# Two transformer blocks on one core: the value slab with the gates in one bank of each pool, its pieces cut 2, 3 and 3

## The chip, the cores and the metric

The kernel runs on one core of one Trainium2 chip, as one program in one launch. The metric is device time in microseconds (us), the median of several executions. Before the change three executions gave 802.09, 802.58 and 803.4 us, so the median is 802.58 us. Engines are named as the profile names them: PE is TensorE (PEld its weight loads), DVE is VectorE, ACT is ScalarE, POOL is GpSimd, and SP is the queue that issues nearly all DMAs.

## The reference

Two blocks run one after the other on 256 tokens of width 1024, all in float32. The first block has differential attention, retention, a squared-ReLU MLP and a gated embedding. The second block has an mLSTM mixer and a gated MLP with a causal convolution of width 3. A last RMS norm closes it. The change touches the entry of the mLSTM mixer only:

```python
def rmsnorm(x, g):
    xf = x.astype(jnp.float32)
    y = xf * lax.rsqrt(jnp.mean(xf * xf, axis=-1, keepdims=True) + EPS) * g.astype(jnp.float32)
    return y.astype(x.dtype)

def mlstm_mixer(x, w_in, b_gates, head_norm, w_out):
    ...
    proj = x @ w_in                      # 1024 -> 512 q, 512 k, 1024 v, 1024 o, 4 + 4 gates
    q = proj[..., :i0].astype(jnp.float32) * (dqk ** -0.5)
    k = proj[..., i0:i1].astype(jnp.float32)
    v = proj[..., i1:i2].astype(jnp.float32)
    o_gate = jax.nn.sigmoid(proj[..., i2:i3].astype(jnp.float32))
    log_i = proj[..., i3:i4].astype(jnp.float32) + bg[:MLSTM_HEADS]
    log_f = jax.nn.log_sigmoid(proj[..., i4:].astype(jnp.float32) + bg[MLSTM_HEADS:])
    ...
```

The eight gate columns give, by running sums and running maxima over the tokens, the decay matrix that weighs q·k before it meets v.

## The kernel before

**Slabs and pieces.** `_plan` cuts every weight matrix into slabs, mostly 8 blocks of 128 rows by 256 columns. A slab comes in pieces: `_rows` says which blocks of rows belong to each. Nearly all slabs have two pieces of four blocks, 128x1024 elements and 512 KB each. The slab `mv0` is wider: 256 columns of v and the 8 gate columns, 264 in all, which is why it has three pieces. The list `order` is the sequence of all pieces; a few pairs of slabs (`JOINT`) have their pieces interleaved. `_packed` lays the weights out in DRAM piece by piece by the same `_rows`.

**A piece's way.** SP loads the piece into one of 5 `raw` buffers (`dma_to`, L155). ACT copies it rounded into one of 6 `hi` buffers (`high_to`, L167). DVE subtracts to get the rest into one of 6 `lo` buffers (`split_to`, L179) and so frees the `raw` buffer, which lets SP load the piece five places on. PE then makes three products per block: weights hi by activations hi, hi by the activations' low part, lo by hi. All engines take their instructions in program order, so an instruction that waits holds back what stands behind it on its engine.

**Order of issue.** `halves` issues the products of a slab piece by piece. After the first piece it runs what is due in the middle (`tails` and the `mid` hooks) and then `slot`, which issues the splits of the pieces ahead and one step of every pending epilogue. `after` does the same at the slab's end.

**PSUM.** The pool `psum` has two rings of 4 banks: `mmbank` ("big products", one bank per slab) and `aux` (everything small: sums, transposes, decay, scores). A new tile takes the bank that was handed out four tiles earlier in its ring, and PE has to wait until that one has been read out.

**The place of the change.** `joint(["mq0", "mk0"], ...)` multiplies the new activations h4 into `ps_mq0` and `ps_mk0`. `step_wide("mv0")` follows, with one bank for each half of the tokens, `ps_mv0_0` and `ps_mv0_1`. After the first piece of `mv0` the tail of the joint step runs: two matmuls with `ones` (`r4_pe`, L1004 and L1005, tile `pv_n4`) sum the squares `sqs_n4` and `sqs_n5`. From them DVE and ACT make the two norms' common factor `rr` (`r4_post`, L1012 to L1020). Only then can DVE read out `ps_mq0` and `ps_mk0`, which need `rr` (`post_scaled`, L561, into `mqk`). Then come `mq1`, `mk1`, `mv1`, `mv2`, `mv3`, `mo0` and so on.

**The gates.** In the middle of `mq1`, `mv0_tail` transposes `rr` to a column on PE (`pc_c5`, L500), DVE copies it (`rrc`, L507), and ACT scales the gate columns of `ps_mv0_0` and `ps_mv0_1` into `gtok` (L1039). In the middle of `mk1` PE transposes them (`pg_t`, L1044). DVE adds the biases (`gi`, `gf`, L1051 and L1052). After `mk1`, `gates2` runs the scans on DVE (L1062 to L1071) and an exponential on ACT (`me`, L1072). After `mv1`, PE transposes `gi` and `me` to columns (`pa_g`, L1082). After `mv2` PE spreads the decay over the tokens (`mm0`, `mm1`, L1100) and makes the first scores (`ms`); DVE builds `dm` from them (L1109).

Of the kernel before, what the change touches and what calls it, by code (L numbers as in the profile page):

```python
# [37 lines left out]
def _plan():  # L38
# [47 lines left out]
    for i in range(len(slabs)):  # L86
        n = slabs[i][0]
        if n not in paired:
            order += [(i, s) for s in range(len(_rows(slabs[i])))]
        elif any(n == g[0] for g in JOINT):  # L90
            order += [(i, 0), (i + 1, 0), (i, 1), (i + 1, 1)]
# [3 lines left out]
def _rows(slab):  # L95

    name, w, k0, nk, cl = slab
    return ((0, 1, 2), (3, 4, 5), (6, 7)) if name == "mv0" else (tuple(range(nk // 2)), tuple(range(nk // 2, nk)))


def _width(slab):
    return 264 if slab[0] == "mv0" else 2048 // slab[3]
# [3 lines left out]
def block_kernel(ctx: ExitStack, tc: tile.TileContext, I, out):  # L106
# [15 lines left out]
    def mmbank(name):  # L122
        return psum.tile([P, 512], F32, tag="mm", name=name)

    def aux(name):
        return psum.tile([P, 512], F32, tag="aux", name=name)
# [10 lines left out]
    slabs, index, order = _plan()  # L137
# [7 lines left out]
    def geometry(i):  # L145
        return len(_rows(slabs[i])[0]), _width(slabs[i])

    def dma_to(n):
        while state["dma"] < min(n, len(order)):
            i, s = order[state["dma"]]  # L150
            name = slabs[i][0]
            kk, cw = len(_rows(slabs[i])[s]), _width(slabs[i])
            raw = wpool.tile([P, 1024], F32, tag="raw", name=f"raw_{name}_{s}", bufs=NRAW)
            v = raw[:, 0:kk * cw].rearrange("p (k n) -> p k n", k=kk)
            nc.sync.dma_start(out=raw[:, 0:kk * cw], in_=I["w"][state["dma"], :, 0:kk * cw])  # L155
            raw_t[i, s] = v
            state["dma"] += 1
# [100 lines left out]
    def after(i, *posts):  # L258

        if i in hooks_pe:  # L260
            drain(i - 1)
            for f in hooks_pe.pop(i):
                f()
        slot()
        for f in list(posts) + hooks_post.pop(i, []):
            later(i, f)

    def halves(i, piece):
        for s in range(len(_rows(slabs[i]))):
            need(i, s)  # L270
            piece(s)
            used.add((i, s))
            if s == 0:
                while tails and i >= tails[0][0]:
                    tails.pop(0)[1]()
                if i in hooks_mid:
                    drain(i - 1)
                    for f, g in hooks_mid.pop(i):
                        f()
                        later(i, g)  # L280
                slot()
# [23 lines left out]
    def step_wide(name, xh, xl):  # L305

        i = index[name]
        kk, cw = geometry(i)
        pss = [mmbank(f"ps_{name}_{t}") for t in range(2)]

        def piece(s):
            for t in range(2):
                ts = slice(t * P, (t + 1) * P)
                for a, k in enumerate(_rows(slabs[i])[s]):
                    hv, lv = hi_t[i, s], lo_t[i, s]
                    o = pss[t][:, 0:cw]
                    TE.matmul(o, lhsT=xh[:, k, ts], rhs=hv[:, a, :], start=k == 0, stop=False, skip_group_check=True)
                    TE.matmul(o, lhsT=xl[:, k, ts], rhs=hv[:, a, :], start=False, stop=False, skip_group_check=True)
                    TE.matmul(o, lhsT=xh[:, k, ts], rhs=lv[:, a, :], start=False, stop=k == 7, skip_group_check=True)

        halves(i, piece)
        after(i)
        return pss
# [42 lines left out]
    with tc.manual_schedule():  # L366
# [93 lines left out]
        for n in range(4):  # L460
            for tag, dt, d in (("hi", F32R, hi_t), ("lo", F32R, lo_t)):
                t = wpool.tile([P, 1024], dt, tag=tag, name=f"{tag}_{n}", bufs=NBUF)
# [262 lines left out]
        i, ps0 = index["q0"], [mmbank(f"ps_{n}") for n in ("q0", "k0")]  # L725
# [192 lines left out]
        for j in range(4):  # L918
            ps = mmbank(f"ps_f2_{j}")
            for kg in range(4):  # L920
                i = index[f"f2_{j}_{kg}"]
# [13 lines left out]
        i = index["wp"]  # L935
# [271 lines left out]
        drain(STAT - 1)  # L1207
        joint(["mq0", "mk0"], h4h, h4l, r4_pe, r4_post, [post_scaled(mqt, 0, rrq), post_scaled(mkt, 0, rr)])
        pss0 = step_wide("mv0", h4h, h4l)
        tails.append((index["mq1"], lambda: mv0_tail(pss0)))  # L1210
        step_b("mq1", h4h, h4l, post_scaled(mqt, 1, rrq))
# [316 lines left out]
```

## Time and profile before

| what | value |
|---|---|
| median of 3 executions | 802.58 us |
| the profiled execution | 802.1 us |
| its span in the profile | 800.3 us |
| PE busy | 786.9 us, 98% of the span |
| DVE busy | 569.9 us, 71% |
| ACT busy | 464.7 us, 58% |
| HBM traffic | 139.68 MB read, 1.05 MB written |
| mean granted PE clock | 0.997 of full speed |

A PE matmul of the usual form is shown with about 281 ns, but matmuls are pipelined: from one start to the next pass about 0.118 us. So stretches of PE are measured from start to start. The span lies 1.8 us below the execution's own time; that rest is outside the program's instructions.

### The profile page before, as it was taken

The numbers are of one execution on the slowest core, as the hardware profiler recorded it, in microseconds if no ns is written. First come the engines' busy times: TensorE is split into PE (matmuls) and PEld (weight loads), VectorE is DVE, ScalarE is ACT, GpSimd is POOL, SyncE is SP. The second block draws the span as 40 slices with busy tenths as digits, with TensorE's granted clock in tenths as the row PEclk, the third lists the DMA queues.
The fourth block names the chain that finished last, engine by engine and source line by source line (L and its number), as shares of the span: only waits on it lengthen the run. The fifth ranks groups of instructions, "written<-read, shape, count | busy, mean of one in ns | idle before, by whom it ended". The sixth has DMA issues, their size and how long they took to land.

```text
span 800.3 us, 15703 instructions
## 1 busy us (share of the span) xinstructions
PE 786.9 (98%) x6394; PEld 772.5 (97%) x6394; DVE 569.9 (71%) x895; ACT 464.7 (58%) x788; POOL 2.2 (0%) x8
## 2 busy tenths in 40 slices
PE   8999999999999999999999999799999999999996
PEld 8999999999999999999999999799999999999885
DVE  6877888556666667666545557887978988987443
ACT  7655657765744446556344456755865766766332
POOL 0000000000000000000000000000000000000000
PEclk9999999999999999999999999999999999999999
DMA  8775544455656556665656544354365456765621
GB/s 302 270 240 158 158 159 130 134 169 169 191 184 187 182 184 188 187 185 194 192 184 186 188 160 149 132 186 156 107 220 175 134 183 219 232 207 162 209 79 53
DMA packets 40472, 141.75 MB, mean 177 GB/s; under 512 B 4640, under 2 KB 5024, under 8 KB 40400
## 3 DMA queue, kind: packets, MB, share of 16 engines
q1 hardware_dynamic: 40032, 140.02, 55.3%
q8 instruction: 50, 0.82, 0.4%
q0 software_dynamic: 224, 0.72, 0.2%
q14 instruction: 22, 0.18, 0.1%
q10 hardware_dynamic: 144, 0.00, 0.0%
HBM read 139.68 MB, written 1.05 MB: 176 GB/s over the span
## 4 chain that ended last, share of the span: by engine, by line
PE 95%; ACT 2%; DMA 1%; DVE 1%; issue 0%; SPq 0%; DVEq 0%; ACTq 0%
PE ps_f L231 8%; PE ps_f L230 8%; PE ps_f L232 8%; PE ps_uv L230 3%; PE ps_ug L230 3%; PE ps_ug L231 3%; PE ps_uv L231 3%; PE acc L1368 3%; PE acc L1366 3%; PE acc L1367 3%; PE ps_ug L232 3%; PE ps_uv L232 3%; PE ps_vr L242 1%; PE ps_va L242 1%; PE ps_mo L242 1%; PE ps_wo L231 1%
## 5 line engine op out<-in xcount | busy, mean ns | idle before, releaser
L179 DVE TENSOR_TENSOR lo_f<-raw_f,hi_f 128x1024 fp32r<-128x1024 f32 x64 | 77.7, 1223 | 52.8 <-ACT hi_f L167 52.8
L167 ACT ACTIVATE hi_f<-raw_f 128x1024 fp32r<-128x1024 f32 x64 | 67.6, 1060 | 79.6 <-PE ps_f L231 70.3
L231 PE MATMUL ps_f<-al,hi_f 128*128 128x256 f32 x256 | 72.1, 282 | 0.0
L230 PE MATMUL ps_f<-ah,hi_f 128*128 128x256 f32 x256 | 72.0, 281 | 0.0
L232 PE MATMUL ps_f<-ah,lo_f 128*128 128x256 f32 x256 | 72.0, 281 | 0.0
L230 PE MATMUL ps_f<-h2h,hi_f 128*128 128x256 f32 x256 | 71.9, 281 | 0.0
L231 PE MATMUL ps_f<-h2l,hi_f 128*128 128x256 f32 x256 | 71.9, 281 | 0.0
L232 PE MATMUL ps_f<-h2h,lo_f 128*128 128x256 f32 x256 | 71.8, 281 | 0.0
L230 PEld LDWEIGHTS ps_f<-ah,hi_f 128*128 128x128 f32 x256 | 48.3, 189 | 0.0
L232 PEld LDWEIGHTS ps_f<-ah,lo_f 128*128 128x128 f32 x256 | 48.3, 189 | 0.0
L230 PEld LDWEIGHTS ps_f<-h2h,hi_f 128*128 128x128 f32 x256 | 48.3, 189 | 0.0
L231 PEld LDWEIGHTS ps_f<-al,hi_f 128*128 128x128 f32 x256 | 48.2, 188 | 0.0
L231 PEld LDWEIGHTS ps_f<-h2l,hi_f 128*128 128x128 f32 x256 | 48.1, 188 | 0.0
L232 PEld LDWEIGHTS ps_f<-h2h,lo_f 128*128 128x128 f32 x256 | 48.1, 188 | 0.0
L179 DVE TENSOR_TENSOR lo_dn<-raw_dn,hi_dn 128x1024 fp32r<-128x1024 f32 x22 | 26.9, 1223 | 22.8 <-ACT hi_dn L167 22.8
L167 ACT ACTIVATE hi_dn<-raw_dn 128x1024 fp32r<-128x1024 f32 x22 | 23.3, 1061 | 30.7 <-PE acc L1367 24.5
L230 PE MATMUL ps_ug<-h7h,hi_ug 128*128 128x256 f32 x144 | 40.8, 283 | 0.0
L230 PE MATMUL ps_uv<-h7h,hi_uv 128*128 128x256 f32 x144 | 40.5, 282 | 0.0
L231 PE MATMUL ps_uv<-h7l,hi_uv 128*128 128x256 f32 x144 | 40.3, 280 | 0.0
L231 PE MATMUL ps_ug<-h7l,hi_ug 128*128 128x256 f32 x144 | 40.3, 280 | 0.0
L232 PE MATMUL ps_ug<-h7h,lo_ug 128*128 128x256 f32 x144 | 40.0, 278 | 0.0
L232 PE MATMUL ps_uv<-h7h,lo_uv 128*128 128x256 f32 x144 | 40.0, 278 | 0.0
(492 smaller groups left out, 2936.6 us busy)
## 6 DMA issues: line engine op xcount, KB each, us to landing
raw_f<-in_w_dram SPq DMA_DIRECT2D x64, 512.0 KB, 4.2
raw_ug<-in_w_dram SPq DMA_DIRECT2D x22, 512.0 KB, 4.4
raw_uv<-in_w_dram SPq DMA_DIRECT2D x22, 512.0 KB, 4.3
raw_dn<-in_w_dram SPq DMA_DIRECT2D x22, 512.0 KB, 3.6
raw_va<-in_w_dram SPq DMA_DIRECT2D x8, 512.0 KB, 4.8
raw_vr<-in_w_dram SPq DMA_DIRECT2D x8, 512.0 KB, 3.5
raw_gr<-in_w_dram SPq DMA_DIRECT2D x8, 512.0 KB, 3.5
raw_ga<-in_w_dram SPq DMA_DIRECT2D x8, 512.0 KB, 3.6
```

The costliest lines, as they stand in the source:

```text
L167: S.activation(hi_t[i, s], raw_t[i, s], ACTF.Copy)
L179: V.tensor_tensor(out=lo_t[i, s], in0=raw, in1=hi_t[i, s].bitcast(F32), op=ALU.subtract)
L230: TE.matmul(o, lhsT=hv[:, a, sl], rhs=xh[:, x, :], start=st, stop=False, skip_group_check=True)
L231: TE.matmul(o, lhsT=hv[:, a, sl], rhs=xl[:, x, :], start=False, stop=False, skip_group_check=True)
L232: TE.matmul(o, lhsT=lv[:, a, sl], rhs=xh[:, x, :], start=False, stop=sp, skip_group_check=True)
L242: TE.matmul(o, lhsT=xh[:, k, ts], rhs=hv[:, a, :], start=st, stop=False, skip_group_check=True)
L1366: TE.matmul(o, lhsT=gh[b][:, r, ts], rhs=hv[:, 0, ns], start=k == 0, stop=False)
L1367: TE.matmul(o, lhsT=gl[b][:, r, ts], rhs=hv[:, 0, ns], start=False, stop=False)
L1368: TE.matmul(o, lhsT=gh[b][:, r, ts], rhs=lv[:, 0, ns], start=False, stop=k == NK - 1)
```

## The change

`ps_mv0_1` is taken from the ring `aux` in place of `mmbank`; `ps_mv0_0` stays in `mmbank`. The pieces of `mv0` hold blocks (0, 1), (2, 3, 4), (5, 6, 7) in place of (0, 1, 2), (3, 4, 5), (6, 7). The width now comes from `_width`, which gives the same 264. No instruction is added or removed on any engine.

```diff
 def _rows(slab):
 
     name, w, k0, nk, cl = slab
-    return ((0, 1, 2), (3, 4, 5), (6, 7)) if name == "mv0" else (tuple(range(nk // 2)), tuple(range(nk // 2, nk)))
+    return ((0, 1), (2, 3, 4), (5, 6, 7)) if name == "mv0" else (tuple(range(nk // 2)), tuple(range(nk // 2, nk)))
...
     def step_wide(name, xh, xl):
 
         i = index[name]
-        kk, cw = geometry(i)
-        pss = [mmbank(f"ps_{name}_{t}") for t in range(2)]
+        cw = _width(slabs[i])
+        pss = [mmbank(f"ps_{name}_0"), aux(f"ps_{name}_1")]
```

In the rows of the program's order below, a name ends in the number of its buffer, and what an instruction waits for stands in brackets.

On PE, after the first piece of `mv0` (its last products are those of `hi_mv0_0` and `lo_mv0_0`), the two sums `pv_n4` follow; this is the difference there:

```order
 L318 MATMUL ps_mv0_1_6302<-hi_mv0_0_6102,h4l_5833 128x264
 L319 MATMUL ps_mv0_1_6302<-lo_mv0_0_6123,h4h_5832 128x264
-L317 MATMUL ps_mv0_1_6302<-hi_mv0_0_6102,h4h_5832 128x264
-L318 MATMUL ps_mv0_1_6302<-hi_mv0_0_6102,h4l_5833 128x264
-L319 MATMUL ps_mv0_1_6302<-lo_mv0_0_6123,h4h_5832 128x264
-L1004 MATMUL pv_n4_6321<-sqs_n4_6199,ones_95 128x256
-L1005 MATMUL pv_n4_6321<-sqs_n5_6205,ones_95 128x256
+L1004 MATMUL pv_n4_6315<-sqs_n4_6199,ones_95 128x256
+L1005 MATMUL pv_n4_6315<-sqs_n5_6205,ones_95 128x256
 L317 MATMUL ps_mv0_0_6301<-hi_mv0_1_6187,h4h_5832 128x264
```

Three products for each half of the tokens, six in all, have gone from ahead of the two sums to the end of `mv0`.

On PE, from the last product of `mv0` to the first ones of `mq1`, and on to the transposes and the first products of `mk1`, before:

```order
L319 MATMUL ps_mv0_1_6302<-lo_mv0_2_6237,h4h_5832 128x264
L230 MATMUL ps_mq1_6382<-h4h_5832,hi_mq1_0_6253 128x256 [waits DVE_49,PE_49,Activation_49]
L231 MATMUL ps_mq1_6382<-h4l_5833,hi_mq1_0_6253 128x256
L232 MATMUL ps_mq1_6382<-h4h_5832,lo_mq1_0_6255 128x256
...
L500 MATMUL pc_c5_6407<-ident_109,rr_6128 128x128 x2
...
L230 MATMUL ps_mk1_6461<-h4h_5832,hi_mk1_0_6338 128x256 [waits DVE_49,PE_49,Activation_49]
```

and on PE at the same place of the changed kernel:

```order
L319 MATMUL ps_mv0_1_6302<-lo_mv0_2_6237,h4h_5832 128x264
L230 MATMUL ps_mq1_6382<-h4h_5832,hi_mq1_0_6253 128x256 [waits Activation_49]
L231 MATMUL ps_mq1_6382<-h4l_5833,hi_mq1_0_6253 128x256
L232 MATMUL ps_mq1_6382<-h4h_5832,lo_mq1_0_6255 128x256 [waits DVE_49]
...
L500 MATMUL pc_c5_6407<-ident_109,rr_6128 128x128 [waits DVE_49]
...
L230 MATMUL ps_mk1_6461<-h4h_5832,hi_mk1_0_6332 128x256 [waits DVE_49,Activation_49]
```

The first product of `mq1` no longer waits for DVE to read a bank out; the third now waits for its `lo` piece, the transposes wait for `rr`, and `mk1` waits for the read-out of `ps_mq0`.

On DVE, behind the two sums of squares `sqs_n4` and `sqs_n5`, this is the difference:

```order
 L435 TENSOR_TENSOR sqs_n5_6205<-sqa_n5_5835 128x256
 L179 TENSOR_TENSOR lo_mv0_1_6207<-raw_mv0_1_5972,hi_mv0_1_6187 128x792
-L179 TENSOR_TENSOR lo_mv0_2_6237<-raw_mv0_2_6007,hi_mv0_2_6235 128x528
+L179 TENSOR_TENSOR lo_mv0_2_6237<-raw_mv0_2_6007,hi_mv0_2_6235 128x792
 L179 TENSOR_TENSOR lo_mq1_0_6255<-raw_mq1_0_6039,hi_mq1_0_6253 128x1024
 L179 TENSOR_TENSOR lo_mq1_1_6297<-raw_mq1_1_6076,hi_mq1_1_6295 128x1024
```

The third piece is larger here by one block of 264 columns, and `lo_mv0_0`, ahead of these rows, is smaller by one. No instruction changes its place on DVE, ACT or SP.

## Rows read from the trace of the kernel before

**Rows 1.** The page: first its line of engines (busy us, share of the span, instructions), then the chain of work that ended last, by engine.

```profile
PE 786.9 (98%) x6394; PEld 772.5 (97%) x6394; DVE 569.9 (71%) x895; ACT 464.7 (58%) x788; POOL 2.2 (0%) x8
...
PE 95%; ACT 2%; DMA 1%; DVE 1%; issue 0%; SPq 0%; DVEq 0%; ACTq 0%
```

**Rows 2.** The waits of PE over the whole span: who waited for whom, us in total, times, longest us.

```profile
PE ps_mq L230 <- ACT hi_mv L167: 3.8, 1, 3.8
...
PE ps_q L230 <- ACT hi L466: 0.9, 2, 0.6
PE ps_mq L230 <- ACT h4h L441: 0.6, 1, 0.6
```

**Rows 3.** The timeline of PE from `mv0` to `mv2`: start us, duration us, engine, line, tiles, shape, and in brackets the idle time before and what ended it. The buffers' numbers are left out, so `mq0` and `mq1` are both `mq`; here it is `mq1`, `mk1`, `mv1` and `mv2`.

```profile
515.02 0.28 PE L319 MATMUL ps_mv<-lo_mv,h4h 128*128 128x264 f32 x1
519.06 0.55 PE L230 MATMUL ps_mq<-h4h,hi_mq 128*128 128x256 f32 x1 [3.76 <-ACT hi_mv L167]
...
522.17 0.28 PE L232 MATMUL ps_mq<-h4h,lo_mq 128*128 128x256 f32 x1
...
523.24 0.28 PE L232 MATMUL ps_mq<-h4h,lo_mq 128*128 128x256 f32 x1
523.36 0.38 PE L500 MATMUL pc_c<-ident,rr 128*128 128x128 f32 x2
...
526.41 0.28 PE L230 MATMUL ps_mk<-h4h,hi_mk 128*128 128x256 f32 x1
...
529.25 0.38 PE L1044 MATMUL pg_t<-ident,gtok 128*64 128x128 f32 x2
...
538.11 0.22 PE L1082 MATMUL pa_g<-ident,gi 4*128 4x4 f32 x1
538.19 0.20 PE L1082 MATMUL pa_g<-ident,me 4*128 4x4 f32 x1
```

**Rows 4.** Stretches of the span: length us, then busy us and instructions of PE, PEld, DVE, ACT and POOL, then the granted clock of PE as a share of 2.4 GHz, the DMA share and GB/s.

```profile
515.20:519.10 3.90, 0.14 (x2) 0.07 (x1) 2.80 (x8) 3.78 (x6) 0.00 (x0) 0.95 0.81 295
519.10:522.20 3.10, 3.10 (x15) 3.10 (x16) 2.68 (x3) 0.84 (x1) 0.00 (x0) 0.51 0.22 26
522.20:538.00 15.80, 15.80 (x135) 15.77 (x134) 12.29 (x20) 8.04 (x16) 0.00 (x0) 1.00 0.67 230
```

**Rows 5.** The timeline of DVE in the same stretch, columns as in rows 3.

```profile
499.26 0.98 DVE L179 TENSOR_TENSOR lo_mv<-raw_mv,hi_mv 128x792 fp32r<-128x792 f32 x1
500.15 0.69 DVE L982 TENSOR_TENSOR pgs<-pgs,pw 128x512 f32<-128x512 f32 x1
...
509.92 0.43 DVE L435 TENSOR_TENSOR sqs_n<-sqa_n 128x256 f32<-128x256 f32 x1
510.27 1.59 DVE L179 TENSOR_TENSOR lo_mv<-raw_mv,hi_mv 128x792 fp32r<-128x792 f32 x2
511.78 2.35 DVE L179 TENSOR_TENSOR lo_mq<-raw_mq,hi_mq 128x1024 fp32r<-128x1024 f32 x2
...
517.43 0.42 DVE L402 TENSOR_TENSOR rr<-nt_n,y_n 128x256 f32<-128x256 f32 x1
...
518.22 0.69 DVE L561 TENSOR_TENSOR mqk<-ps_mq,rrq 128x512 f32<-128x512 f32 x1
...
519.42 2.35 DVE L179 TENSOR_TENSOR lo_mk<-raw_mk,hi_mk 128x1024 fp32r<-128x1024 f32 x2
523.77 0.16 DVE L507 COPY rrc<-pc_c 128x2 f32<-128x2 f32 x1 [2.00 <-PE pc_c L500]
...
529.67 0.47 DVE L1051 TENSOR_SCALAR gi<-pg_t,par 4x256 f32<-4x256 f32 x1 [0.93 <-PE pg_t L1044]
...
530.66 2.36 DVE L179 TENSOR_TENSOR lo_mv<-raw_mv,hi_mv 128x1024 fp32r<-128x1024 f32 x2
```

**Rows 6.** The timeline of ACT: the first and the third piece of `mv0` with what follows each, and the exponential of the gates.

```profile
492.99 0.87 ACT L167 ACTIVATE hi_mv<-raw_mv 128x792 fp32r<-128x792 f32 x1 [1.18 <-PE ps_pg L231]
493.77 1.69 ACT L441 ACTIVATE h4h<-x,gfg 128x256 fp32r<-128x256 f32 x4
...
509.07 0.63 ACT L167 ACTIVATE hi_mv<-raw_mv 128x528 fp32r<-128x528 f32 x1
509.60 1.99 ACT L167 ACTIVATE hi_mq<-raw_mq 128x1024 fp32r<-128x1024 f32 x2
...
536.69 0.42 ACT L1072 ACTIVATE me<-gl 4x256 f32<-4x256 f32 x1 [3.25 <-DVE gl L1071]
```

**Rows 7.** The timeline of PE in the joint step and in `mv0`, columns as in rows 3.

```profile
501.30 0.28 PE L232 MATMUL ps_mk<-h4h,lo_mk 128*128 128x256 f32 x1
502.16 0.38 PE L230 MATMUL ps_mq<-h4h,hi_mq 128*128 128x256 f32 x1 [0.58 <-ACT h4h L441]
...
508.46 0.29 PE L317 MATMUL ps_mv<-hi_mv,h4h 128*128 128x264 f32 x1
...
510.64 0.59 PE L1004 MATMUL pv_n<-sqs_n,ones 128*128 128x256 f32 x2
...
511.31 0.47 PE L317 MATMUL ps_mv<-hi_mv,h4h 128*128 128x264 f32 x1
```

**Rows 8.** From issue to landing of the five loads of `raw_mv` (512 KB each) that are issued between 511 and 525 us.

```profile
DMA to landing us min/median/max: 3.6/4.8/5.1
```

**Rows 9.** The timeline of DVE after the decay products of PE, columns as in rows 3.

```profile
545.14 2.69 DVE L1109 SCALAR_TENSOR_TENSOR dm<-mm,acol,maskT 128x256 f32<-128x256 f32 x8 [1.33 <-PE mm L1101]
```

## The prediction

> **What bounds the kernel now.** I read the page first. PE is busy for 98% of the span, and the chain of work that ended last is 95% PE [rows 1]. So the end moves only when a pause of PE is shortened or its products run faster. The waits of PE name all pauses there are [rows 2]: one of 3.8 us ahead of a product into `ps_mq`, one of 0.6 us in the joint step, and some at the program's start, which the change does not touch. The timeline of PE puts the long one between the last product of `mv0` at 515.02 and the first of `mq1` at 519.06 [rows 3]. The view gives an ACT copy, `hi_mv`, as the releaser, but the order of the program shows that product waiting for DVE too, and DVE is what fits: its read-out of `ps_mq0` begins at 518.22 and takes 0.69, to 518.91 [rows 5]. `mq1` needs a fifth bank of a ring of four (`ps_mq0`, `ps_mk0` and two of `mv0` hold them), and the oldest cannot be read out before `rr` is known. The pause has a second price: from 519.1 to 522.2 PE's clock was granted at 0.51, the 1.2 GHz level, and after that again at 1.00, 2.4 GHz [rows 4].
>
> **The change part by part.**
>
> *The pause at mq1.* With `ps_mv0_1` in the other ring `mq1` takes a free bank, and its first product has no wait for DVE left. What it cost: a product of `mv0` passes in about 0.12, so PE was free at 515.14, and the pause is 519.06 - 515.14 = 3.92. The slow clock: from 519.06 to 522.17 there are 14 starts in 3.11; at the pace right after it, (523.24 - 522.17)/9 = 0.119 [rows 3], they take 1.66, so 1.45 more. Together 5.37. What is late next at this place: `hi_mq1` and `lo_mq1` are done by 514.13 in the old times (511.78 + 2.35 [rows 5]), so nothing.
>
> *The smaller first piece.* On ACT `hi_mv0_0` with 792 columns takes 0.78 to the next start, one with 528 takes 0.53 [rows 6]: 0.25 less. On DVE `lo_mv0_0` takes 0.89 to the next start; the pair of 792 and 528 takes 511.78 - 510.27 = 1.51, so the smaller one 0.62 [rows 5]: 0.27 less. Both stand ahead of the splits of h4 and of the sums of squares, on a chain where each instruction waits for the one before, so `sqs_n5` ends 0.52 earlier, 509.83 in place of 510.35 [rows 5]. PE's pause in the joint step (501.30 to 502.16, of which 0.58 counted as a wait for h4h [rows 7]) shrinks by the same 0.52, and `mv0` starts at 507.94 in place of 508.46 [rows 7]. The two sums now come after 12 products, at 509.39, and the second, 0.43 later, meets `sqs_n5` about in time. Next PE needs `lo_mv0_1`, which DVE ends at 510.7; here about 0.3 of the lead is lost, by waiting for it and for the second sum. I let `mv0` end 0.24 earlier: 514.90.
>
> *The larger third piece* puts 0.27 back on DVE ahead of `r4_post`. Net of the 0.52, `rr` is 0.25 earlier: 517.60 in place of 517.85 [rows 5]. The six products moved behind the sums are still made; they cost nothing more.
>
> *PE from there.* 0.24 + 5.37 = 5.61 earlier. `mq1`'s first half of 24 products ends at 514.90 + 24 x 0.118 = 517.73, and the transposes `pc_c5` find `rr` just ready (517.60). This is a new wait by the order, and it has only 0.13 to spare. `mk1` starts at 526.41 - 5.61 = 520.80 [rows 3] and takes the bank of `ps_mq0`, read out at 518.66: 2.1 to spare. The transposes `pa_g` would stand at 538.11 - 5.61 = 532.50.
>
> *What is late next: the gates.* `pa_g` needs `me`, and `me` comes off the DVE queue, which does not gain 5.61. DVE gains the 0.25; then its 2.00 wait for `pc_c5` and its 0.93 wait for `pg_t` [rows 5], since both transposes now come earlier than DVE gets to them (the splits of `mk1` end at 519.42 - 0.25 + 2.35 = 521.5, `pc_c5` at about 518.1; DVE asks for `pg_t` at 529.67 - 0.93 - 2.25 = 526.5, and PE makes it at 529.25 - 5.61 = 523.6). Sum 3.18. `me` is ready at 536.69 + 0.42 = 537.11 [rows 6], hence at 533.93. Before, its first use at 538.19 [rows 3] left 1.08 to spare; now PE is there at 538.19 - 5.61 = 532.58 and pauses for 1.4. What gets through is 5.61 - 1.4 = 4.2. The raw loads keep up with this: a load takes at most 5.1 to land [rows 8], the load of `mv2_1` goes out behind `lo_mk1_0` (the first half of the 2.35 above) at about 520.4 and is there by 525.5, its copy by 526.6, and DVE wants it at 530.66 - 3.18 = 527.5 [rows 5]. That is 0.9 to spare, and `mv3_0` has about as much.
>
> *After the gates* DVE is 1.0 later against PE than it was, but at the decay it used to wait 1.33 for PE [rows 9], so that cover is just enough. From there all engines follow PE as before, and no PE wait stands behind it in rows 2. The 4.2 reaches the end.
>
> *The bank in the other ring.* `ps_mv0_1` stays there until DVE has made `mvl`, behind the splits of `mv1`. Its next owner, by the ring's order, is `pa_g`. In the old times `lo_mv1` could start at 523.77 [rows 5] and needs about 2.3, `mvl` 0.9 more, so 527 at the latest, against 538.11. Cost nothing; cover over 10 us.
>
> **A short pause and the clock** is what I cannot price from one row. A pause of 3.92 was followed by the 1.2 GHz level for 3.1 us [rows 4]; the pause of 0.86 in the joint step [rows 7] was not, as the next starts are at the normal pace. The new pause of 1.4 lies between. If the clock stays, it costs 0; if it falls as after the long one, 1.45. I take 0, by the nearer row. The Trainium skill speaks for the other end: its page "TensorE: Matmul & The Clock Gate", section "A second HAM failure mode: psum-queue depth-cycling", tells of a kernel in which short pauses of PE between groups of products that rotate through PSUM banks made the clock fall again and again. By that the time would be the 799.9 of the second rival below; no run here shows a pause of this length.
>
> **The sum.** Against the profiled execution's own time: 802.1 - 4.2 = 797.9. That execution lay 0.48 below the median of the runs shown (802.58), so for a median I write 798.3.
>
> **The rivals.**
> 1. The gates keep up (DVE or ACT have more room than I count, or `me` comes sooner), and the whole 5.6 gets through: 802.58 - 5.6 = 797.0. For it: DVE idles elsewhere in this stretch. Against: its queue from the splits of `mk1` to the scans has no other pause.
> 2. The clock falls after the pause at `pa_g`: 4.2 - 1.45 = 2.75, so 799.9.
> 3. The gates do not come forward: the two waits of DVE (2.00 and 0.93) turn into waits for raw loads that land late or for ACT's copies. Then `me` comes at about 536.9, PE's lead is used up at `pa_g`, and 0.25 + 1.08 = 1.3 are left: 801.3, no change that can be told. The 0.9 to spare of the loads speaks against it. That the change does not do what it says, `mq1` waiting still, would give 802.4; the order of the program excludes it nearly.
> 4. Slower: the clock. PE now runs close behind DVE through the whole mLSTM mixer, and pauses at `pa_g`, the decay, the scores and the products with v. Each fall costs 1.45. With three the gain is gone (4.35 against 4.2); it is slower by more than 0.2% from four falls on, each with some 0.3 of pause: 802.58 - 4.2 + 4 x 1.75 = 805.4. Against it: the cover at the decay, and one pause at most by my count.
>
> **How the numbers follow.** Forecast (a gain of 3.4 to 5.0) 0.56, rival 1 0.18, rival 2 0.14, rival 3 with the unchanged wait 0.08, rival 4 0.04. About 0.2%, 1.6 us, is what a measurement of this kernel can tell from no change. Faster by more: 0.56 + 0.18 + 0.14 = 0.88; within it 0.08; slower 0.04. The range takes in the forecast and rivals 1 and 2, with 0.4 to 0.5 for the scatter of the runs: 796.6 to 800.4.
>
> **What the profile of the changed kernel would show.** The 3.8 wait at `mq1` is gone from PE's waits, and the granted clock stays full behind 515. `mv0` starts near 507.9 and `mq1` near 514.9, with starts 0.118 apart. DVE copies `rrc` without a wait for `pc_c5`, at about 521.5, and reads `pg_t` without one. PE has one new wait of about 1.4 at `pa_g`, L1082, released by ACT's `me`, and `mv2` starts some 4.2 earlier than before. The forecast is wrong if a wait shows at `pc_c5` or `mk1` of over 0.5, if stretches behind `pa_g` show 1.2 GHz, if `pa_g` has no wait (rival 1), or if PE waits for a `lo` piece of `mv1`, `mv2` or `mv3`.

## The result, and the profile after

The changed kernel takes 797.94 us (median of 4 runs, 797.67 to 798.03) against 802.89 us (4 runs, 802.09 to 803.4) of the kernel before on the same chip: a ratio of 0.9939, 95% interval 0.9921 to 0.9956. It is faster by 0.6%. Forecast were 798.3 and a range of 796.6 to 800.4. The profiled execution took 797.67, its span is 795.9; before it was 800.3, so the two traces differ by 4.4.

The page's line of engines, after (as the first line of [rows 1]):

```profile
PE 785.8 (99%) x6394; PEld 771.2 (97%) x6394; DVE 569.5 (72%) x895; ACT 464.6 (58%) x788; POOL 2.2 (0%) x8
```

The same instructions, and PE with 10.1 us of the span not busy in place of 13.4. The waits of PE, after, columns as in [rows 2]:

```profile
PE warm L388 <- DVE epst L385: 1.1, 1, 1.1
PE pa_g L1082 <- ACT me L1072: 1.0, 1, 1.0
PE ps_q L230 <- ACT hi L466: 0.9, 2, 0.5
```

The 3.8 ahead of `mq1` is gone, and so is the 0.6 in the joint step. One wait is new: 1.0 at `pa_g`, for the gates' `me`. The rest belongs to the program's start. The timeline of PE, after, answers to [rows 3] and [rows 7]; the rows are the start of `mv0`, its two sums, its last product, then `mq1`, the transposes `pc_c5`, `mk1`, the transposes of the gates, `pa_g` and the first product of `mv2`:

```profile
507.94 0.29 PE L317 MATMUL ps_mv<-hi_mv,h4h 128*128 128x264 f32 x1
...
509.40 0.59 PE L1004 MATMUL pv_n<-sqs_n,ones 128*128 128x256 f32 x2
...
514.87 0.28 PE L319 MATMUL ps_mv<-lo_mv,h4h 128*128 128x264 f32 x1
514.99 0.28 PE L230 MATMUL ps_mq<-h4h,hi_mq 128*128 128x256 f32 x1
...
517.83 0.38 PE L500 MATMUL pc_c<-ident,rr 128*128 128x128 f32 x2
...
520.90 0.28 PE L230 MATMUL ps_mk<-h4h,hi_mk 128*128 128x256 f32 x1
...
523.73 0.38 PE L1044 MATMUL pg_t<-ident,gtok 128*64 128x128 f32 x2
...
532.59 0.22 PE L1082 MATMUL pa_g<-ident,gi 4*128 4x4 f32 x1
533.78 0.22 PE L1082 MATMUL pa_g<-ident,me 4*128 4x4 f32 x1 [0.97 <-ACT me L1072]
534.05 0.38 PE L242 MATMUL ps_mv<-hi_mv,h4h 128*128 128x256 f32 x1
```

`mq1` follows `mv0` at once, 4.07 earlier than before. By `pa_g` PE is 5.52 earlier (532.59 against 538.11 in [rows 3]), which is the pause with its slow clock and the shorter joint step. Then it waits 1.1, start to start beyond the usual 0.09, and what is left is 4.4. The windows of the span, after, columns as in [rows 4]:

```profile
515.00:517.60 2.60, 2.60 (x25) 2.60 (x24) 1.56 (x4) 2.54 (x4) 0.00 (x0) 1.00 0.91 358
517.60:521.00 3.40, 3.40 (x31) 3.40 (x30) 3.33 (x6) 2.10 (x3) 0.00 (x0) 1.00 0.10 37
...
532.00:534.50 2.50, 1.53 (x13) 1.30 (x12) 1.64 (x5) 1.19 (x3) 0.00 (x0) 1.00 0.44 167
534.50:540.00 5.50, 5.50 (x48) 5.37 (x46) 5.38 (x7) 3.24 (x6) 0.00 (x0) 1.00 0.55 191
540.00:610.00 70.00, 69.91 (x581) 69.31 (x581) 56.66 (x121) 49.36 (x105) 0.00 (x0) 1.00 0.49 152
```

The clock stays at 1.00 in all of them, that after the new pause included; [rows 4] had 0.51 for 3.1 us. The timeline of DVE, after, answers to [rows 5] and, with its last row, to [rows 9]:

```profile
509.39 0.42 DVE L435 TENSOR_TENSOR sqs_n<-sqa_n 128x256 f32<-128x256 f32 x1
...
517.18 0.43 DVE L402 TENSOR_TENSOR rr<-nt_n,y_n 128x256 f32<-128x256 f32 x1
...
521.44 0.15 DVE L507 COPY rrc<-pc_c 128x2 f32<-128x2 f32 x1
...
526.30 0.46 DVE L1051 TENSOR_SCALAR gi<-pg_t,par 4x256 f32<-4x256 f32 x1
...
540.74 2.69 DVE L1109 SCALAR_TENSOR_TENSOR dm<-mm,acol,maskT 128x256 f32<-128x256 f32 x8 [0.86 <-PE mm L1101]
```

`rrc` and `gi` carry no bracket any more: the two waits of DVE for PE (2.00 and 0.93) are gone, so the gates come 3.4 earlier (`gi` 526.30 against 529.67). That is 2.1 less than PE's 5.5. One row of ACT's timeline, after, ends the chain:

```profile
533.31 0.41 ACT L1072 ACTIVATE me<-gl 4x256 f32<-4x256 f32 x1 [3.76 <-DVE gl L1071]
```

`me` is there at 533.72, 3.4 earlier than before (537.11), and `pa_g` goes on at 533.78. Of the 2.1 that PE gained more than `me`, 1.08 is what `me` had to spare before; the rest is the new pause.

A measure without the program's ends is used below: the **stage**, from the first sum `pv_n3` (PE, L957) to the first sum `pv_n6` (L1253). Before it lasts 614.54 - 481.18 = 133.36, after 610.12 - 481.13 = 128.99: 4.37 less, nearly all of the difference of the spans. The rows of PE's timeline, before and then after:

```profile
481.18 0.59 PE L957 MATMUL pv_n<-sqs_n,ones 128*128 128x256 f32 x2
...
614.54 0.59 PE L1253 MATMUL pv_n<-sqs_n,ones 128*128 128x256 f32 x2
```

```profile
481.13 0.59 PE L957 MATMUL pv_n<-sqs_n,ones 128*128 128x256 f32 x2
...
610.12 0.59 PE L1253 MATMUL pv_n<-sqs_n,ones 128*128 128x256 f32 x2
```

### The profile page after: what moved, and what is told of

Same layout as the page of the kernel before. It is cut to its first block, busy times and chain, and to the rows that moved or that the text cites. A ratio compares the mean times of both kernels' runs of the same rounds, so it can differ in the third digit from the quotient of the medians.

```text
span 795.9 us, 15702 instructions
## 1 busy us (share of the span) xinstructions
PE 785.8 (99%) x6394; PEld 771.2 (97%) x6394; DVE 569.5 (72%) x895; ACT 464.6 (58%) x788; POOL 2.2 (0%) x8
## 4 chain that ended last, share of the span: by engine, by line
PE 94%; DVE 3%; ACT 1%; DMA 1%; issue 1%; SPq 0%; DVEq 0%
PE ps_f L231 8%; PE ps_f L230 8%; PE ps_f L232 8%; PE ps_uv L230 3%; PE ps_ug L230 3%; PE ps_uv L231 3%; PE ps_ug L231 3%; PE acc L1368 3%; PE acc L1366 3%; PE acc L1367 3%; PE ps_ug L232 3%; PE ps_uv L232 3%; PE ps_vr L242 1%; PE ps_wo L231 1%; PE ps_va L242 1%; PE ps_mo L242 1%
```

## The experiments

The theory is the prediction's: the bank does nearly all (pause and slow clock go), the pieces give some 0.25, and a part of the gain is held back at `pa_g` by DVE's queue. The rivals: the pieces do more; the bank lent from the small ring brings a wait of its own; the pause and the slow clock are one cost and not two; the pause at `pa_g` covers something else, so that its removal gives nothing. The first four experiments ran on one chip (the kernel before: 802.48, 15 runs), the other three on another (802.52, 14 runs).

**The bank alone.** The changed kernel with the old pieces:

```diff
-    return ((0, 1), (2, 3, 4), (5, 6, 7)) if name == "mv0" else (tuple(range(nk // 2)), tuple(range(nk // 2, nk)))
+    return ((0, 1, 2), (3, 4, 5), (6, 7)) if name == "mv0" else (tuple(range(nk // 2)), tuple(range(nk // 2, nk)))
```

> The bank of the small ring with the old pieces (3, 3, 2). If the free bank is what gave the gain, the pause at mq1 is gone here too: mv0 starts at 508.4 and ends at 515.1, rr is ready at 517.85, and the gates' me comes 0.25 to 0.3 later than in the changed kernel, so the time is 0.25 above it: about 798.2 where the changed kernel has 797.9. If instead the smaller first piece is needed (rr would come too late for the transposes pc_c5 and PE would pause there), PE shows a new pause of over 0.5 at pc_c5 and the time is above 799.

Measured: 798.17 (798.04 to 798.28), ratio 0.9943 (0.9931 to 0.9956). The stage lasts 610.49 - 481.25 = 129.24, 4.12 less than before and 0.25 more than after. The waits of PE:

```profile
PE ps_q L230 <- ACT hi L466: 1.5, 2, 1.1
PE pa_g L1082 <- ACT me L1072: 1.1, 1, 1.1
...
PE ps_mq L230 <- ACT h4h L441: 0.6, 1, 0.6
```

The 3.8 is gone without the pieces, no pause shows at `pc_c5`, `pa_g` waits as in the changed kernel, and the 0.6 in the joint step is back. The slow clock is gone too (a window, columns as in [rows 4]):

```profile
515.00:518.00 3.00, 3.00 (x28) 3.00 (x27) 1.93 (x6) 2.60 (x4) 0.00 (x0) 1.00 0.95 339
```

**The pieces alone.** The changed kernel with both sums of `mv0` in the big ring:

```diff
-        pss = [mmbank(f"ps_{name}_0"), aux(f"ps_{name}_1")]
+        pss = [mmbank(f"ps_{name}_{t}") for t in range(2)]
```

> The new pieces (2, 3, 3) with both sums in the ring of the big products. If the free bank gave the gain, the pause at mq1 stays: mv0 ends near 514.9, mq1 waits until ps_mq0 is read out at 518.66, so 3.8 of pause, then some 14 products at 1.2 GHz; only 0.25 is gained, about 802.6. If the smaller first piece were worth its full 0.5 at the end, or the clock did not fall this time, it would be 802.3 or 801.2.

Measured: 802.30 (801.89 to 803.37), ratio 0.9997 (0.9988 to 1.0006): no difference that the times can tell. The trace tells one: the stage lasts 614.35 - 481.21 = 133.14, 0.22 less than before. The pause stays; the timeline of PE, and the two waits of DVE:

```profile
518.89 0.55 PE L230 MATMUL ps_mq<-h4h,hi_mq 128*128 128x256 f32 x1 [3.65 <-ACT hi_mv L167]
```

```profile
DVE rrc L507 <- PE pc_c L500: 2.0, 1, 2.0
DVE gi L1051 <- PE pg_t L1044: 0.9, 1, 0.9
```

By the stage the parts add up: 4.12 for the bank, 0.22 for the pieces, 4.37 for both.

**The gates late.** The changed kernel with the products of `pa_g` and what follows them moved from the end of `mv1` into the middle of `mv2`, some 3 us further back on PE:

```diff
-        at("mv1", gates3_pe, gates3_post)
+        at("mv2", gates3_pe, gates3_post, mid=True)
```

> The changed kernel, with the transposes pa_g of the gates moved from the end of mv1 to the middle of mv2 (24 products later, 2.8 us). If the changed kernel is held back only by the wait for me at pa_g (1.1 of pause), that pause goes and nothing else on PE waits: 1.1 less than the changed kernel, about 796.8, as dm still finds its column acol in time (DVE waited 0.86 for PE there). If DVE is the bound of the whole stretch, the wait comes back at the decay or at the first products with v, and the time stays at 797.9.

Measured: 797.61 (797.42 to 797.88), ratio 0.9937 (0.9924 to 0.9949), which is nearer to the rival's 797.9 than to the theory's 796.8. Yet the pause at `pa_g` is gone, and the stage lasts 609.72 - 481.63 = 128.09, which is 0.90 less than after. The answer was left between the two, so it was run again beside a second run of the changed kernel (below).

**Both sums in the small ring.** The changed kernel with `ps_mv0_0` there as well:

```diff
-        pss = [mmbank(f"ps_{name}_0"), aux(f"ps_{name}_1")]
+        pss = [aux(f"ps_{name}_{t}") for t in range(2)]
```

> Both sums of mv0 in the small ring, none in the ring of the big products, so mk1 finds a free bank as well. If the gates hold the changed kernel, the time is the same (797.9, the pause at pa_g stays at about 1.0). If the banks of the big products were still the limit (mk1 takes the bank of ps_mq0), it is faster; if the small ring is now short, PE shows a pause at pg_t, pa_g or the decay and it is slower by that.

Measured: 797.84 (797.68 to 798.07), ratio 0.994 (0.9927 to 0.9952); the stage lasts 610.51 - 481.50 = 129.01. The waits of PE:

```profile
PE warm L388 <- DVE epst L385: 1.1, 1, 1.1
PE pa_g L1082 <- ACT me L1072: 1.0, 1, 1.0
PE ps_q L230 <- ACT hi L466: 0.4, 1, 0.4
```

A second bank lent from the small ring brings no wait there, and a second one freed in the big ring gives nothing: one bank was lacking.

**The pause filled.** The kernel before, with 28 products that nobody reads behind `mv0`, so that PE is busy where it paused:

```diff
         pss0 = step_wide("mv0", h4h, h4l)
+        fill = aux("fill")
+        for _ in range(28):
+            TE.matmul(fill[:, 0:T], lhsT=h4h[:, 0, 0:P], rhs=h4h[:, 0, :], start=True, stop=True)
```

> The kernel before, with 28 products more between mv0 and mq1 whose sum nobody reads; they only keep PE at work for 28 x 0.118 = 3.3 of the 3.9 us of the pause. If the 1.2 GHz stretch behind the pause comes from PE's idling, it is gone: mq1 still starts at 519.0, but its products pass in 0.118, and 1.45 less than the kernel before remain, about 801.0. If the clock fell for another reason (the loads or the read-outs of that moment), the stretch stays and the time is that of the kernel before, 802.5.

Measured: 800.89 (800.73 to 801.18), ratio 0.9977 (0.9968 to 0.9987). The timeline of PE, and two windows, columns as in [rows 4]:

```profile
515.35 3.51 PE L1212 MATMUL fill<-h4h 128*128 128x256 f32 x28
...
519.25 0.36 PE L230 MATMUL ps_mq<-h4h,hi_mq 128*128 128x256 f32 x1 [0.39 <-ACT hi_mv L167]
```

```profile
515.20:518.50 3.30, 3.30 (x30) 3.30 (x29) 2.19 (x7) 2.99 (x5) 0.00 (x0) 1.00 0.89 318
519.20:522.20 3.00, 2.95 (x25) 2.98 (x26) 2.77 (x3) 0.94 (x1) 0.00 (x0) 1.00 0.09 30
```

`mq1` starts no earlier (519.25 where the stage began 0.19 later than before), but its products run at full clock, 25 in 3.0 us in place of 15 in 3.1. Only the clock was given back: 802.52 - 800.89 = 1.63 in the time, and 133.36 - (613.34 - 481.37) = 1.39 in the stage.

**The changed kernel again, and the gates late again**, one beside the other, with nothing edited in the one and the edit of the gates in the other.

> The changed kernel once more, as it is, beside the next one on the same chip: 797.9 by either theory.

> The kernel with pa_g in the middle of mv2 once more. In the trace of its first run the stretch from the sum pv_n3 to the transposes tu_m was 0.9 shorter than in the changed kernel, while the medians differ by 0.3. If the 0.9 is real and the rest the scatter of the program's start, the time is 0.5 to 1.0 below the changed kernel beside it. If something behind the mixer takes it back, both stretches end equal and the times agree within 0.3.

Measured: 797.86 (797.61 to 797.98), ratio 0.9939 (0.9925 to 0.9952), and 797.49 (797.34 to 797.62), ratio 0.9934 (0.9922 to 0.9947). The gates late are 0.37 faster, between the 0.5 to 1.0 of the one expectation and the at most 0.3 of the other; the runs of the two overlap only from 797.61 to 797.62. In the stage the difference is larger: 610.25 - 481.25 = 129.00 against 609.52 - 481.47 = 128.05, or 0.95. With the gates late, the timeline of PE has `pa_g` without a pause and a short wait at the first product of the scores with v:

```profile
535.79 0.22 PE L1082 MATMUL pa_g<-ident,gi 4*128 4x4 f32 x1
535.88 0.20 PE L1082 MATMUL pa_g<-ident,me 4*128 4x4 f32 x1
...
550.20 0.36 PE L555 MATMUL my<-mvh,ws_m 128*128 128x258 f32 x1 [0.19 <-DVE w_m L544]
```

In the same kernel the timeline of DVE shows why something is asked back there: the 0.86 for which DVE waited ahead of the decay is used up.

```profile
540.14 2.67 DVE L1109 SCALAR_TENSOR_TENSOR dm<-mm,acol,maskT 128x256 f32<-128x256 f32 x8
```

So the pause at `pa_g` held back 1.1; without it PE gains 0.95, and DVE takes the rest at the scores. Less of the 0.95 reaches the time: 0.37 by the medians, and 0.2 in the two traced executions, whose spans are 796.0 and 795.8. In these two the stage began 0.22 later (481.47 against 481.25), and the last store took longer. Its issue on SP, in the changed kernel and with the gates late:

```profile
792.81 0.38 SPq L1422 DMA_DIRECT2D out_dram<-xtok  x1
```

```profile
792.08 0.38 SPq L1422 DMA_DIRECT2D out_dram<-xtok  x1
```

So 3.2 pass from the issue to the end of the span in the one and 3.7 in the other. In the earlier run of the same edit it was issued at 792.28 of a span of 796.1, which is 3.8; in the other seven traces, the kernel before among them, it is 3.2. The DMA view from that issue on shows what differs. First the changed kernel (KB, and us from issue to landing, stand at the end), then the gates late, where one packet of the queue that the view calls instruction (packets, MB, share of the 16 engines) falls into the store:

```profile
out_dram<-xtok SPq DMA_DIRECT2D x1, 256.0 KB, 2.3
```

```profile
q14 instruction: 1, 0.01, 0.5%
...
out_dram<-xtok SPq DMA_DIRECT2D x1, 256.0 KB, 2.8
```

In both traces with the gates late this packet starts 1.3 behind the issue of the last store; in the other seven traces the last packet of that queue starts 1.5 to 1.8 ahead of it. That the packet is what holds the store up is likely and not shown, as no run moved it alone; why it comes later with the gates late stays open.

## Why the prediction was right

**The pause at mq1 and its clock (5.37).** Right, and they are two costs. With the bank alone the wait and the 0.51 are both gone; with the pause filled, the clock alone is given back, 1.39 to 1.63 for the 1.45 of the prediction. The bank alone also shows the releaser: with a free bank `mq1` starts at once, while with the pause filled it starts at the same place in the stage as before, the view naming `hi_mv` as ever. What held it was the bank, as the order said, and not the copy that the view names: in the changed kernel that copy begins on ACT only after `mq1` has started (514.99).

```profile
517.71 1.99 ACT L167 ACTIVATE hi_mv<-raw_mv 128x1024 fp32r<-128x1024 f32 x2
```

**The smaller first and the larger third piece.** Right to 0.1: `mv0` starts at 507.94 (507.94 was written), `sqs_n5` ends at 509.81 (509.83), `mv0` ends at about 514.99 (514.90), `rr` at 517.61 (517.60). `pc_c5` stands at 517.83 and finds `rr` ready with 0.2 to spare (0.13). By itself this gives 0.22 (0.25), which no time can tell.

**The gates.** Right in mechanism, with a term mis-sized: the gain on DVE was written as 3.18 and is 3.4. `rrc` comes 2.33 earlier (2.25), and `gi` 3.37 (3.18). The brackets count a wait from the end of the instruction ahead; without a wait each of the two now starts 0.08 before that end (`rrc` at 521.44, where the splits of `mk1` end at 521.52). So `me` is there at 533.72 and not at 533.93, while PE asks for it at 532.68 and not at 532.58. The pause is 1.1 and not 1.4, and 4.4 get through and not 4.2.

**After the gates.** The cover of DVE at the decay was to shrink from 1.33 to 0.3; 0.86 is left. DVE is indeed 1.0 later against PE, but one more wait is gone, for ACT's `hi_mo` between the gates and the decay, which the prediction did not count. It stood in the timeline of DVE before, and the same line of code has no such wait after:

```profile
542.59 1.23 DVE L179 TENSOR_TENSOR lo_mo<-raw_mo,hi_mo 128x1024 fp32r<-128x1024 f32 x1 [0.46 <-ACT hi_mo L167]
```

```profile
538.68 1.20 DVE L179 TENSOR_TENSOR lo_mo<-raw_mo,hi_mo 128x1024 fp32r<-128x1024 f32 x1
```

That it is cover, and just enough, the gates late show: there it is all used up, and PE waits 0.2 at the scores.

**The loads and the lent bank (0).** Right: no `lo` piece of `mv1`, `mv2` or `mv3` shows among the waits of PE, `gi` came forward in full, and lending even two banks brought no wait. One copy on ACT, by the order of the pieces that of `mv3_0`, waits for its load now; it is done at 527.11, and DVE comes to that piece only at about 528.4, so this costs nothing:

```profile
526.05 1.06 ACT L167 ACTIVATE hi_mv<-raw_mv 128x1024 fp32r<-128x1024 f32 x1 [0.73 <-DMA raw_mv<-in_w_dram]
```

**The short pause and the clock (0, and not 1.45).** Right: PE idle for about 1.1 at `pa_g` is followed by a granted clock of 1.00. The Trainium skill, page "TensorE: Matmul & The Clock Gate", section "A second HAM failure mode: psum-queue depth-cycling", tells of a kernel whose frequent short idles between groups of products make the clock swing; had that held for a single pause, the second rival's 799.9 would have come. In this kernel one pause of 1.1 does not do it, one of 3.8 does; what a series of short ones would do, no run here shows.

**The rivals.** The first (the gates keep up, 797.0) falls by the wait at `pa_g` in the trace; the second by the clock (its own sum, 802.58 - 2.75, gives 799.8); the third by the missing brackets at `rrc` and `gi`; the fourth as no stretch behind `pa_g` has a lower clock.

**The time.** By the traces 4.4 was gained, by the medians 4.66 (802.52 less 797.86) and 4.95 (802.89 less 797.94), each pair on one chip. The profiled execution of before, at 802.1, is among its quickest. The runs of the two kernels that have the long pause (before and the pieces alone) lie over 1.3 to 1.6 us; those of the others, the one with the filled pause among them, over 0.2 to 0.5. The mean granted clock of each execution goes with it: of the 29 executions of the kernel before that ran beside the experiments, the ten that took 803.0 or more had 0.993 or 0.994, and the nineteen at 802.8 or less had 0.995 to 0.997. So the long executions are those with more of the slow clock, and the medians gain a little more than the traces by losing it. Where in such an execution the slow clock lies was not seen, as none of these is among the traces; and one of the pieces alone, 803.37 with 0.946, is not explained.

For the same reason the prediction's last step went a little too far: the 0.4 that it added to its 797.9 is scatter of the kernel with the pause, while the changed kernel's median lies 0.27 above its profiled execution (797.94 and 797.67). Of the 0.36 between the forecast of 798.3 and the result, 0.13 comes from there and 0.23 from the gain that was written too small.

## What to carry to other kernels

When a pause of an in-order engine is removed, look for the next result that it needs from the other engines' queues and count what they gain by themselves; the difference to what the engine gains, less what that result had to spare before, is the new pause. Here 5.5 became 4.4 since the gates, standing in DVE's queue, gained only 3.4 and had 1.1 to spare; moving their user some 3 us further back gave another 0.95 in the stage and 0.37 in the time, 797.49 against 797.86 and 802.52, the fastest version of these. A pause that lets the clock fall has a second price, which can be measured alone by filling the pause with work that nobody reads, and a shortage of one buffer in a ring can be shown by lending one, or two, from a neighbour.

## What was not expected of the hardware

The clock came as the prediction took it: after the 3.8 pause it was at 0.51 for 3.1 us, after 1.1 at 1.00 throughout; so removing a pause can be worth more than its length. Not expected was that the scatter goes with it: without the long pause the executions of a kernel lie within 0.5 us, with it within 1.3 to 1.6, the longer ones at a lower mean clock. And two kernels with the same last instructions differ in what passes between the issue of the last store and the end of the span, 3.2 against 3.7 and 3.8, enough to hide half of a gain of 0.9; where it is longer, a packet of the instruction queue falls into the store.
